# Recurrent mixer: gate matmuls in row-tile pairs, weights split by casting and accumulating DMAs, and a quarter of x turned by DMA

## The chip, the cores and the metric

One core of one Trainium2 chip runs the whole kernel. The metric is the device time of one execution in microseconds (us). Of the engines, PE is TensorE (PEld its weight loads), DVE VectorE, ACT ScalarE, POOL GpSimd, SP SyncE; DMAs are issued from the queues of SP, POOL and ACT.

## What is computed

Two layers, 512 positions, width 1024, everything in float32. Each layer is: half a SwiGLU feed-forward (inner width 2816), a token mixer, another half feed-forward, each behind an RMS norm and added to x. Layer 0's mixer is the Griffin recurrence, layer 1's a spatial gating unit. The change lies in layer 0's mixer and at the entry of the feed-forward behind it:

```python
def block_diag_linear(x, w, b):            # 16 heads of 64
    xh = x.reshape(bsz, s, h, dh)
    return (jnp.einsum('bshi,hij->bshj', xh, w) + b).reshape(bsz, s, h * dh)

def rg_lru(x, w_a, b_a, w_x, b_x, lam):
    gate_a = jax.nn.sigmoid(block_diag_linear(xf, w_a, b_a))
    gate_x = jax.nn.sigmoid(block_diag_linear(xf, w_x, b_x))
    log_a = -LRU_C * gate_a * jax.nn.softplus(-lam)
    a = jnp.exp(log_a)
    bx = xf * gate_x * jnp.sqrt(-jnp.expm1(2.0 * log_a))
    # h[t] = a[t] * h[t-1] + bx[t]

def recurrent_mixer(...):
    y, r = jnp.split(x @ w_in, 2, axis=-1)
    y = jax.nn.gelu(y)
    r = causal_depthwise_conv(r, conv_w, conv_b)      # width 4
    return (y * rg_lru(r, ...)) @ w_out
```

## The kernel before

**Three matmuls for one product.** Each float32 operand is split into a high and a low part of type float32r: hi is a ScalarE copy, lo a VectorE subtraction (source - hi). A product is then hi x hi + hi x lo + lo x hi, three matmuls into one PSUM bank (`mm3`, lines 247 to 250). Weights come from HBM by DMA into `raw` tiles (512 KB, ten buffers, `RAW_BUFS`), and `Sub.split` (from line 194) makes `whi` and `wlo` of them. The feed-forwards and output products use a seven-product scheme (named P1 to P7 and Q4) on quarters A11, A12, A21, A22 of the left side and sums of them (S1 to S4); these are `seven` and `out_blocks`. In that scheme a raw buffer is often changed in place: an accumulating DMA from POOL adds another weight block (`Raw.add`, line 161), either right after the load (`plus`, some blocks later) or after the first split (`then`).

**The order.** The program is a list `subs` of blocks; each has one raw buffer and its matmuls. The loop at the end of `trunk` goes through them. For block i it runs the accumulating loads that are due, the hook phase "pre", the split of block i + 3 (`SPLIT_AHEAD`), the phases "mid" and "rest", the loads for which buffers have come free (`load_more`), block i's matmuls, "end", the block's post-processing, and "late". Every engine runs its instructions in the order in which this loop issued them; the schedule is manual. So a hook at a block and phase fixes an instruction's place in its engine's queue.

**The recurrence** (`recurrent`, from line 1203). Its 1024 r columns and 1024 y columns are eight chunks of 128 each; below, r0 to r7 and y0 to y7 are their blocks. r0 to r3 come as two halves of 256 positions each, all first halves and then all second halves; r4 to r7, then y0 to y7, have 24 matmuls of 512 columns each. Behind a chunk r of the convolution's input there is, for chunk c: `rc` on ScalarE (the last tap and the bias, out of PSUM) and three taps on VectorE; a split of rc into hi and lo; the gate matmuls (`gate`); two sigmoids out of PSUM and a tanh (`sigmoids`, giving g and tl); `pr` = rc x gate_x on VectorE. Later hooks (`plan`) run the exponentials, `oma2` (two VectorE instructions on tl for 1 - a^2), the square roots, and the scans. Behind y there are gelus on ScalarE, and `yh` multiplies y by h.

**The gates before.** For two chunks of heads and each of the gates a and x a tile of 128 x 512 is cleared by a POOL memset, and 64 x 64 blocks are loaded on its block diagonal (`load_gate`, line 1206). The four tiles are split. Each chunk has one 128-row `mm3` per gate, half of whose weights are zeros: six matmuls of 512 columns, two banks. There are 48 of them.

**The output product and the norm.** y7 is followed by 14 blocks of 12 matmuls: P1, P5, P2 for the first cut of the left side, the same for the second, then P6, P3, P6, P3, P7, P7, Q4, Q4. When a quarter of x is final, `BlockNorm.quarter` arranges for its turning: `Group.stage` has TensorE transpose 128 x 128 pieces (eight for a quarter, line 294) into a PSUM bank, ScalarE evicts them with the norm's gains (`take`), and `parts` splits them. `BlockNorm` can do without TensorE for the quarters named in `cross`: `Group.rows` has ScalarE spread the 16-bit halves of x into planes (`pl`), SP transposes them by DMA (`dt`), ScalarE merges the halves, and the gains are applied in the later sums and splits. The feed-forwards around use it; the recurrence's `BlockNorm` has no `cross`. The first block of the next feed-forward (P1) needs A11's parts.

Of the kernel before, what the change touches and what calls it, by code (L numbers as in the profile page):

```python
# [14 lines left out]
P = 128  # L15
# [20 lines left out]
SPLIT_AHEAD = 3  # L36
SLOTS = 56
V_AT = 1, 7, 9, 10
WS_AT, WS_MERGE = 90, 8
# [36 lines left out]
def trunk(ctx: ExitStack, tc: tile.TileContext, a: dict, out: bass.AP):  # L76
# [57 lines left out]
    class Raw:  # L134


        halves = False

# [20 lines left out]

        def add(self, src):  # L160
            nc.gpsimd.dma_start(out=self.v, in_=src, accum_op=ALU.add)  # L161

# [11 lines left out]
    class Sub:  # L174
# [93 lines left out]
    def vcol(row):  # L268
        return vec[:, row : row + 1]
# [933 lines left out]
    def recurrent(w_in, w_out, norm):  # L1203
        gates = {}

        def load_gate(name, q):
            g = gates[name, q] = slot(name="gw")
            nc.gpsimd.memset(g, 0.0)
            gv = g.rearrange("p (c j) -> p c j", c=4)
            wv = a[f"rec_gate_{name}_w"][0, q * 8 : (q + 1) * 8].rearrange("(c two) i j -> two i c j", two=2)  # L1210
            for two in range(2):
                nc.sync.dma_start(out=gv[two * 64 : (two + 1) * 64, :, two * 64 : (two + 1) * 64], in_=wv[two])

        def split_gate(name, q):
            gates[name, q] = split(gates[name, q])

        at0 = len(subs)
        y0 = at0 + 12
        for n, (name, q) in enumerate((name, q) for q in range(2) for name in ("a", "x")):
            hook(at0 + (-9,-8,-2,-1)[n], "late", lambda name=name, q=q: load_gate(name, q))  # L1220
            hook(at0 + (-3,-2,3,4)[n], "mid", lambda name=name, q=q: split_gate(name, q))

        rc, ga, gx, tl, pr, ym = {}, {}, {}, {}, {}, {}

        def r_post(c, ps):
            n = now[0]
            g = n + (2 if c < 4 or c == 6 else 1)
            v = rc[c] = slot(name="rc")
# [27 lines left out]
            hook(n, "late", taps)  # L1256
            hook(n + 1, "mid", lambda: hl.extend(split(v)))
            hook(g, "end", gate)
# [56 lines left out]
        plan(1, "late", (exp_, 5, 6, 7), (oma2, 5, 6, 7))  # L1315
        plan(2, "rest", (sqrt, 5, 6, 7))
        plan(2, "late", (gelu, 0, 1, 2), (scan, 5, 6, 7))
        plan(3, "rest", (yh, 0, 1))
# [24 lines left out]
        def mk(c0, post, halves):  # L1343

            raw = raw_of(w_in[:, c0 : c0 + P].rearrange("(k p) c -> p k c", p=P), [P, KD, P])
            st = {}

# [8 lines left out]

            last = lambda: post(st[0])
            if not halves:
# [309 lines left out]
    def vec_rest():  # L1668

        nc.vector.memset(stage[:V_ROWS, :P], 0.0)  # L1670
        for src, r0, n in rows:
            flat = src.rearrange("h d -> (h d)") if len(src.shape) == 2 else src.rearrange("o h d -> (o h d)")
            nc.gpsimd.dma_start(out=stage[r0 : r0 + n, :P], in_=flat.rearrange("(n p) -> n p", p=P))

# [148 lines left out]
```

## Time and profile before

| | us |
|---|---|
| median of 3 runs | 1559.81 |
| lowest, highest | 1559.05, 1560.93 |
| the profiled execution | 1559.84 |
| its span | 1557.0 |
| TensorE busy in the span | 1549.4 |
| DVE, ACT, POOL busy | 1310.5, 1197.0, 245.6 |
| 48 gate matmuls, first and last start | 350.9 to 391.8 |

The granted TensorE clock is full throughout. In the profile's rows a start is in us from the span's start, and the number behind it is the recorded duration, in which matmuls overlap. In a row of groups, `out<-in xcount` stands for the tiles written and read and how often. A row of a tile's view gives the shortest, the median and the longest duration in ns.

### The profile page before, as it was taken

What the parts mean: (1) busy time and instruction counts of PE and PEld (TensorE: products, weight loads), DVE (VectorE), ACT (ScalarE), POOL (GpSimd) and SP (SyncE); (2) the same over time, 40 slices, a digit from 0 to 9 for tenths busy, and PEclk for the clock granted to TensorE, in tenths of its full rate; (3) what the DMA queues carried; (4) which work ended last, traced back from release to release, by engine and by line L of the source; (5) the groups of instructions that cost most, each with busy time, mean ns of one, the idle gap of its engine ahead of it and who ended that gap; (6) DMA issues with size and microseconds to landing.
All of it is one profiled execution on the core that took longest, in us unless ns stands there. A gap on an engine that the chain in (4) does not pass through costs nothing.

```text
span 1557.0 us, 20941 instructions
## 1 busy us (share of the span) xinstructions
PE 1549.4 (100%) x7237; PEld 1314.8 (84%) x7237; DVE 1310.5 (84%) x1792; ACT 1197.0 (77%) x1789; POOL 245.6 (16%) x220
## 2 busy tenths in 40 slices
PE   9999999999999999999999999999999999999998
PEld 7888888898888998888889988888888889888886
DVE  6977789888999787789897877798879997777998
ACT  7877786668778868786787787867887877777866
POOL 2111112300021111112211211122111111111120
PEclk9999999999999999999999999999999999999999
DMA  9988898953395988899987898989978869898994
GB/s 315 189 189 194 187 219 225 225 146 108 99 235 136 190 199 198 186 237 217 233 212 181 201 219 184 223 229 236 233 200 212 203 141 218 195 210 180 242 234 135
DMA packets 275098, 312.09 MB, mean 200 GB/s; under 512 B 117568, under 2 KB 155568, under 8 KB 274992
## 3 DMA queue, kind: packets, MB, share of 16 engines
q1 hardware_dynamic: 220704, 211.59, 47.6%
q0 software_dynamic: 52496, 97.33, 36.9%
q10 hardware_dynamic: 1792, 1.84, 0.4%
q8 instruction: 56, 0.92, 0.2%
q14 instruction: 50, 0.41, 0.1%
HBM read 282.39 MB, written 2.10 MB: 183 GB/s over the span
## 4 chain that ended last, share of the span: by engine, by line
PE 98%; DVE 1%; DMA 1%; issue 0%; ACT 0%; SPq 0%
PE A L484 15%; PE A L483 15%; PE A L485 15%; PE C L483 8%; PE C L485 8%; PE C L484 8%; PE B L484 4%; PE B L485 4%; PE B L483 4%; PE r L248 2%; PE r L250 2%; PE r L249 2%; PE Q L483 1%; PE Q L485 1%; PE Q L484 1%; PE p L963 1%
## 5 line engine op out<-in xcount | busy, mean ns | idle before, releaser
L110 DVE TENSOR_TENSOR wlo<-raw,whi 128x1024 fp32r<-128x1024 f32 (+2 forms) x567 | 651.1, 1152 | 208.8 <-ACT whi L119 203.6
L119 ACT ACTIVATE whi<-raw 128x1024 fp32r<-128x1024 f32 (+2 forms) x567 | 564.3, 1001 | 226.8 <-DVE raw L110 91.6
L483 PE MATMUL A<-whi,hi 128*128 128x512 f32 (+1 forms) x1104 | 420.9, 381 | 0.0
L484 PE MATMUL A<-whi,lo 128*128 128x512 f32 (+1 forms) x1104 | 419.4, 380 | 0.1
L485 PE MATMUL A<-wlo,hi 128*128 128x512 f32 (+1 forms) x1104 | 419.2, 380 | 0.0
L484 PEld LDWEIGHTS A<-whi,lo 128*128 128x128 f32 x1104 | 207.3, 188 | 36.0 <-DVE lo L110 1.0
L483 PEld LDWEIGHTS A<-whi,hi 128*128 128x128 f32 x1104 | 207.2, 188 | 36.0 <-ACT c L119 1.0
L485 PEld LDWEIGHTS A<-wlo,hi 128*128 128x128 f32 x1104 | 207.2, 188 | 35.6
L483 PE MATMUL C<-whi,hi 128*128 128x512 f32 (+1 forms) x608 | 231.5, 381 | 0.0
L484 PE MATMUL C<-whi,lo 128*128 128x512 f32 (+1 forms) x608 | 231.4, 381 | 0.0
L485 PE MATMUL C<-wlo,hi 128*128 128x512 f32 (+1 forms) x608 | 231.3, 380 | 0.0
L161 POOL DMA_DIRECT2D raw<-in_ffn_w_in_dram x100 | 120.7, 1207 | 697.4 <-DVE raw L110 331.5
L161 POOL DMA_DIRECT2D raw<-in_ffn_w_out_dram x73 | 83.8, 1195 | 318.3 <-DVE wlo L110 203.3
L110 DVE TENSOR_TENSOR raw<-raw,raw 128x1024 f32<-128x1024 f32 (+1 forms) x113 | 130.9, 1158 | 1.1
L484 PEld LDWEIGHTS C<-whi,lo 128*128 128x128 f32 x608 | 114.1, 188 | 20.4 <-DVE lo L110 0.4
L485 PEld LDWEIGHTS C<-wlo,hi 128*128 128x128 f32 x608 | 114.1, 188 | 19.9
L483 PEld LDWEIGHTS C<-whi,hi 128*128 128x128 f32 x608 | 114.1, 188 | 19.9
L110 DVE TENSOR_TENSOR lo<-a,hi 128x512 fp32r<-128x512 f32 (+1 forms) x180 | 116.3, 653 | 0.7 <-ACT hi L119 0.7
L119 ACT ACTIVATE c<-A 128x512 f32<-128x512 f32 (+1 forms) x150 | 81.8, 567 | 45.6 <-PE A L485 45.3
L119 ACT ACTIVATE hi<-a 128x512 fp32r<-128x512 f32 (+1 forms) x180 | 105.4, 595 | 14.4 <-DVE a L110 12.8
L484 PE MATMUL B<-whi,lo 128*128 128x512 f32 (+1 forms) x304 | 115.7, 381 | 0.1
L483 PE MATMUL B<-whi,hi 128*128 128x512 f32 (+1 forms) x304 | 115.7, 381 | 0.0
(189 smaller groups left out, 1974.0 us busy)
## 6 DMA issues: line engine op xcount, KB each, us to landing
raw<-in_ffn_w_in_dram SPq DMA_DIRECT2D x143, 512.0 KB, 5.6
raw<-in_ffn_w_out_dram SPq DMA_DIRECT2D x98, 512.0 KB, 6.0
raw<-in_ffn_w_in_dram POOLq DMA_DIRECT2D x76, 512.0 KB, 7.5
raw<-in_ffn_w_out_dram POOLq DMA_DIRECT2D x58, 512.0 KB, 8.6
raw<-in_ffn_w_in_dram SPq DMA_DIRECT2D x48, 384.0 KB, 4.3
raw<-in_sg_w_in_dram SPq DMA_DIRECT2D x20, 512.0 KB, 9.0
raw<-in_ffn_w_in_dram POOLq DMA_DIRECT2D x24, 384.0 KB, 6.2
raw<-in_rec_w_in_dram SPq DMA_DIRECT2D x16, 512.0 KB, 5.1
```

What stands on the lines that cost most here:

```text
L110: nc.vector.tensor_tensor(out=o, in0=x, in1=y, op=op)
L119: nc.scalar.activation(out=o, in_=x, func=f, **k)
L161: nc.gpsimd.dma_start(out=self.v, in_=src, accum_op=ALU.add)
L248: nc.tensor.matmul(ps, wh, xh, start=start, stop=False)
L249: nc.tensor.matmul(ps, wh, xl, start=False, stop=False)
L250: nc.tensor.matmul(ps, wl, xh, start=False, stop=stop)
L483: nc.tensor.matmul(ps, zh, wh, start=fresh and i == 0, stop=False, **k)
L484: nc.tensor.matmul(ps, zl, wh, start=False, stop=False, **k)
L485: nc.tensor.matmul(ps, zh, wl, start=False, stop=end, **k)
L963: nc.tensor.matmul(bank_of(half, s), z, (sub.lo if m == 2 else sub.hi)[:, q, :], start=left[2] == "2" and (h, q, m) == (0, 0, 0), stop=lef ...
```

## The change

- **Gates.** `load_gate` now fills one tile per chunk of four: for rows 0 to 63 (the even head) the columns hold gate a's block and then gate x's, for rows 64 to 127 (the odd head) gate x's and then gate a's. There are no zeros, no memset, and two tiles in place of four to load and to split. A chunk's gates are three pairs of matmuls; in a pair one matmul uses rows 0 to 63 and the other rows 64 to 127, each into its own bank. Each bank then holds half of both gates, so there are four sigmoids on 64 partitions in place of two on 128, and gate x's bias is loaded with its halves exchanged.
- **Places.** `GATE` puts the gates of most chunks a block later. Chunks 4 to 7 have hi of rc made by VectorE (`OWN_HI`). The first exponentials come one block later; those of chunks 5 to 7, their roots and scans also move by a phase or a block.
- **Casting loads.** For r4 to r7 and y0 to y5 a second DMA from POOL reads the same weights again and casts them into a tile `rawhi`; ScalarE's copy `whi` is dropped and VectorE makes wlo from raw and rawhi. Each such block holds two of the ten buffers, and rawhi until its matmuls are done, so later loads come later.
- **Accumulating loads.** For y6 and y7 (`BELOW`) only rawhi is loaded. Two blocks later ScalarE writes -hi into `rawlo`, and an accumulating DMA from POOL adds the weights: VectorE has no part in it.
- **x's quarter A11** behind the recurrence goes the way of `cross`.

```diff
+GATE = (3, 3, 3, 2, 2, 2, 2, 2)
+OWN_HI = 4
+BELOW = {6: 2, 7: 2}
...
         def load(self):
             _, k, c = self.shape
+            if self.below:
+                self.h, self.l = (rawp.tile([P, 1024], F32R, tag="raw", name=nm(x)).rearrange("p (k c) -> p k c", k=k)
+                                  for x in ("rawhi", "rawlo"))
+                live.update(((self, "hi"), (self, "lo")))
+                nc.gpsimd.dma_start(out=self.h, in_=self.src)
+                pending.append((now[0] + self.below, self))
+                pending.sort(key=lambda p: p[0])
+                return
...
+            if self.cast:
+                self.h = rawp.tile([P, 1024], F32R, tag="raw", name=nm("rawhi")).rearrange("p (k c) -> p k c", k=k)
+                live.add((self, "hi"))
+                nc.gpsimd.dma_start(out=self.h, in_=self.src)
...
         def add(self, src):
+            if self.below:
+                act(self.l, f32(self.h), AF.Copy, scale=-1.0)
+                nc.gpsimd.dma_start(out=self.l, in_=self.src, accum_op=ALU.add)
+                return
...
+            if self.raw.below:
+                self.hi, self.lo = self.raw.h, self.raw.l
+                return
             src = self.raw.v
+            if self.raw.cast:
+                self.hi = self.raw.h
+                _, k, c = src.shape
+                self.lo = wp.tile([P, 1024], F32R, tag="wlo", name=nm("wlo")).rearrange("p (k c) -> p k c", k=k)
+                tt(self.lo, src, f32(self.hi), ALU.subtract)
+                self.raw.used()
+                return
...
-            g = n + (2 if c < 4 or c == 6 else 1)
+            g = n + GATE[c]
...
             def gate():
-                for name in "ax":
-                    pg = bank("gate")
-                    wh, wl = gates[name, c // 4]
-                    cs = slice((c % 4) * P, (c % 4 + 1) * P)
-                    mm3(pg, wh[:, cs], wl[:, cs], hl[0], hl[1], True, True)
-                    pss.append(pg)
+                pss.extend(bank("gate") for _ in range(2))
+                cs = slice((c % 4) * P, (c % 4 + 1) * P)
+                for m in range(3):
+                    for two in range(2):
+                        rows = slice(two * 64, (two + 1) * 64)
+                        nc.tensor.matmul(pss[two], gates[c // 4][m == 2][rows, cs], hl[0][m == 1][rows, :],
+                                         start=m == 0, stop=m == 2)
                 hl.clear()
...
-                for dst, brow in ((ga, V_GA), (gx, V_GX)):
-                    dst[c] = slot(name="g")
-                    act(dst[c], pss.pop(0), AF.Sigmoid, bias=vcol(brow + c))
+                for dst, brow, n in ((ga, V_GA, 0), (gx, V_GX, 1)):
+                    g = dst[c] = slot(name="g")
+                    for two in range(2):
+                        o = (two ^ n) * 64
+                        act(g[two * 64 : (two + 1) * 64], pss[two][o : o + 64], AF.Sigmoid, bias=vcol(brow + c)[o : o + 64])
...
-        plan(-2, "rest", (exp_, 0, 1, 2, 3, 4), (oma2, 0, 1))
+        plan(-1, "rest", (exp_, 0, 1, 2, 3, 4), (oma2, 0, 1))
...
-    recurrent(a["rec_w_in"][0], a["rec_w_out"][0], BlockNorm(V_F2, True, wait=("A12",)))
+    recurrent(a["rec_w_in"][0], a["rec_w_out"][0], BlockNorm(V_F2, True, wait=("A12",), cross={"A11": (((1, "pre"), (4, "rest"), (5, "rest")), ((1, "rest"), (5, "mid"), (6, "mid")))}))
...
-        while loaded < n and len(live) < RAW_BUFS:
+        while loaded < n and len(live) < RAW_BUFS - raws[loaded].cast:
```

Three places show how instructions move. First TensorE, at chunk 1's gate; before, between the last matmuls of a block r and the first of the next (gate is the PSUM bank, its operands are the split gate weights and the split rc):

```order
L250 MATMUL r_3547<-zh_3086,wlo_3391 128x512
L248 MATMUL gate_3572<-hi_3486,hi_3112 128x512
L249 MATMUL gate_3572<-lo_3487,hi_3112 128x512
L250 MATMUL gate_3572<-hi_3486,lo_3113 128x512
L248 MATMUL gate_3576<-hi_3486,hi_3134 128x512
L249 MATMUL gate_3576<-lo_3487,hi_3134 128x512
L250 MATMUL gate_3576<-hi_3486,lo_3135 128x512
L248 MATMUL r_3603<-zh_3058,whi_3429 128x512
```

The same engine and kind of place after the change:

```order
L279 MATMUL r_3512<-zh_3082,wlo_3377 128x512
L1273 MATMUL gate_3537<-hi_3414,hi_3110 128x512
L1273 MATMUL gate_3538<-hi_3414,hi_3110 128x512
L1273 MATMUL gate_3537<-lo_3415,hi_3110 128x512
L1273 MATMUL gate_3538<-lo_3415,hi_3110 128x512
L1273 MATMUL gate_3537<-hi_3414,lo_3111 128x512
L1273 MATMUL gate_3538<-hi_3414,lo_3111 128x512
L277 MATMUL r_3570<-zh_3054,rawhi_3000 128x512
```

The six matmuls now alternate between two banks, each reading 64 rows of the same tiles; the block behind them reads rawhi from the casting load in place of whi. Second ScalarE, from the last roots (tl) through the gelus (y); before:

```order
L119 ACTIVATE tl_3861<-tl_3861 128x512
L119 ACT_TABLE_LOAD
L119 ACTIVATE y_3949<-r_3799 128x512
L119 ACTIVATE y_3951<-r_3874 128x512
L119 ACTIVATE y_3953<-r_3924 128x512
L119 ACTIVATE whi_3964<-raw_3398 128x1024
L119 ACTIVATE hi_4001<-a_850_3968 128x512
L119 ACTIVATE whi_4005<-raw_3437 128x1024
L119 ACTIVATE y_4009<-r_3976 128x512
```

After:

```order
L122 ACTIVATE y_3942<-r_3849 128x512
L122 ACTIVATE y_3944<-r_3912 128x512
L122 ACTIVATE rawlo_3847<-rawhi_3846 128x1024
L122 ACTIVATE hi_3992<-a_838_3959 128x512
L122 ACTIVATE y_3997<-r_3967 128x512
L122 ACTIVATE hi_4005<-a_845_3999 128x512
L122 ACTIVATE whi_4037<-raw_3908 128x1024
```

The splits of y6 and y7 (the two whi rows) have gone; y7's copy into rawlo stands where y6's split stood, right behind the third gelu. Third POOL's queue through the recurrence; before:

```order
L1208 MEMSET gw_3154 128x512
L1208 MEMSET gw_3182 128x512
L161 DMA raw_3545<-in_rec_w_out_dram 128x2x512
L161 DMA raw_3741<-in_rec_w_out_dram 128x2x512
L161 DMA raw_3974<-in_rec_w_out_dram 128x2x512
L161 DMA raw_3545<-in_rec_w_out_dram 128x2x512
```

After, from the casting load of y5 on:

```order
L166 DMA rawhi_3713<-in_rec_w_in_dram 128x8x128
L155 DMA rawhi_3783<-in_rec_w_in_dram 128x8x128
L155 DMA rawhi_3846<-in_rec_w_in_dram 128x8x128
L178 DMA rawlo_3784<-in_rec_w_in_dram 128x8x128
L178 DMA rawlo_3847<-in_rec_w_in_dram 128x8x128
L180 DMA raw_3910<-in_rec_w_out_dram 128x2x512 x2
L180 DMA raw_4048<-in_rec_w_out_dram 128x2x512
```

Twelve casting loads and two accumulating ones stand ahead of the first accumulating load of the output product, and the second of those (`raw_4048`, P5's second cut) now stands behind both loads into P5's first buffer (`raw_3910`).

More of the change, by code (lines that the diff above doesn't have):

```diff
@@ L134, in trunk @@
     class Raw:
-        halves = False
+        halves = cast = below = False
         def __init__(self, src, shape, plus=None, wait=2):
@@ L1204, in recurrent, with load_gate, split_gate @@
         gates = {}
[L1206 to L1208 removed]
+        def load_gate(q):
+            g = gates[q] = slot(name="gw")
             gv = g.rearrange("p (c j) -> p c j", c=4)
[L1210 to L1215, printed above, removed]
+            for n, name in enumerate("ax"):
+                wv = a[f"rec_gate_{name}_w"][0, q * 8 : (q + 1) * 8].rearrange("(c two) i j -> two i c j", two=2)
+                for two in range(2):
+                    o = (two ^ n) * 64
+                    nc.sync.dma_start(out=gv[two * 64 : (two + 1) * 64, :, o : o + 64], in_=wv[two])
+        def split_gate(q):
+            gates[q] = split(gates[q])
         at0 = len(subs)
         y0 = at0 + 12
[L1219 to L1221 removed]
+        for q in range(2):
+            hook(at0 + (-9, -2)[q], "late", lambda q=q: load_gate(q))
+            hook(at0 + (-3, 3)[q], "mid", lambda q=q: split_gate(q))
         rc, ga, gx, tl, pr, ym = {}, {}, {}, {}, {}, {}
@@ L1256, in r_post, with parts @@
             hook(n, "late", taps)
-            hook(n + 1, "mid", lambda: hl.extend(split(v)))
+            def parts():
+                hi, lo = slot(F32R, "hi"), slot(F32R, "lo")
+                if c < OWN_HI:
+                    act(hi, v, AF.Copy)
+                else:
+                    nc.vector.tensor_copy(hi, v)
+                tt(lo, v, f32(hi), ALU.subtract)
+                hl.append((hi, lo))
+            hook(n + 1, "mid", parts)
             hook(g, "end", gate)
@@ L1345, in mk @@
             raw = raw_of(w_in[:, c0 : c0 + P].rearrange("(k p) c -> p k c", p=P), [P, KD, P])
+            raw.cast = not halves
+            raw.below = BELOW.get(c0 // P, 0)
             st = {}
@@ L1355, in mm_of, with last @@
                 return mm
-            last = lambda: post(st[0])
+            def last():
+                live.difference_update(((raw, "hi"), (raw, "lo")))
+                post(st[0])
             if not halves:
@@ L1672, in vec_rest @@
             flat = src.rearrange("h d -> (h d)") if len(src.shape) == 2 else src.rearrange("o h d -> (o h d)")
-            nc.gpsimd.dma_start(out=stage[r0 : r0 + n, :P], in_=flat.rearrange("(n p) -> n p", p=P))
+            v = flat.rearrange("(n p) -> n p", p=P)
+            if r0 == V_GX:
+                for o in (0, 64):
+                    nc.gpsimd.dma_start(out=stage[r0 : r0 + n, o : o + 64], in_=v[:, 64 - o : 128 - o])
+            else:
+                nc.gpsimd.dma_start(out=stage[r0 : r0 + n, :P], in_=v)
     def vec_rest_t():
```

10 lines of the change are left out of this document (7 added, 3 removed).

## The prediction

> **What bounds the kernel now.** I read the page first (busy time, chain), then what TensorE waits for, then its instructions in order of time.
>
> ```profile
> span 1557.0 us, 20941 instructions
> PE 1549.4 (100%) x7237; PEld 1314.8 (84%) x7237; DVE 1310.5 (84%) x1792; ACT 1197.0 (77%) x1789; POOL 245.6 (16%) x220
> ...
> PE 98%; DVE 1%; DMA 1%; issue 0%; ACT 0%; SPq 0%
> ```
> ```profile
> PE warm L1660 <- DVE warm L1655: 1.3, 1, 1.3
> ```
>
> TensorE is busy throughout, holds 98% of the chain that ended last, and its only listed wait is the warm-up's. So the time is the sum of TensorE's matmul intervals, and anything else counts only where it makes TensorE stand. A busy TensorE is still not a measure of an instruction's price, since matmuls overlap in the records; the price is the distance from start to start. The timeline of TensorE around the first gate shows it:
>
> ```profile
> 350.83 0.28 PE L250 MATMUL r<-zh,wlo 128*128 128x256 f32 x1
> 350.95 0.40 PE L248 MATMUL gate<-hi,hi 128*128 128x512 f32 x1
> 351.18 0.40 PE L249 MATMUL gate<-lo,hi 128*128 128x512 f32 x1
> ...
> 352.33 0.28 PE L248 MATMUL r<-zh,whi 128*128 128x256 f32 x1
> ```
>
> A 512-column matmul is recorded with 0.39 us, but the next starts 0.23 us later; a 256-column one takes 0.12 us. The six matmuls of one gate run from 350.95 to 352.33: 1.38 us, and all eight gates 11.0 us.
>
> **The gates.** After the change a gate is three pairs. A pair's two matmuls each use 64 of the 128 rows and write different banks. If the two run at once, a pair costs one 512-column interval, 0.23 us. It also needs two weight loads, and the 256-column matmul above shows that a load with its matmul goes through in 0.12 us: two loads set a floor of 0.24 us per pair. That makes 3 x 0.24 = 0.72 us per gate and 5.8 us for eight: 5.2 us saved at best. The trace has no 64-row matmul, so a price is unknown: what going from whole-array to half-array matmuls and back costs. The most it should cost is the overlap of neighbours, 0.39 - 0.23 = 0.16 us. There are 14 such switches, not 16, since the gates of chunks 2 and 3 stand next to each other. That is 0 to 2.2 us, and with no row nearer to either end I take half, 1.1 us. The saving is then 5.2 - 1.1 = 4.1 us.
>
> The Trainium skill, page TensorEngine Tiling (Array Packing), Key Properties, states that a change of the tiling mode drains TensorE; no run here shows it yet. By that rule the whole 2.2 us is paid and the sum below is 1.1 us worse.
>
> **The turned quarter.** The chain of waits in order of time has the transposes of x's quarter A11:
>
> ```profile
> 457.50 0.87 PE e L294 x8
> ```
>
> Those eight transposes leave TensorE: 0.9 us. What replaces them is on ScalarE, SyncE's queue and VectorE:
>
> ```profile
> L119 ACT ACTIVATE pl<-x x16: 613/614/632, 737.5 to 1090.2; 128x512 uint16<-128x512 uint16 x16
> ```
> ```profile
> L119 ACT ACTIVATE a<-dt x82: 682/1172/1197, 59.0 to 1461.7; 128x1024 uint16<-128x1024 uint16 x70, 128x512 uint16<-128x512 uint16 x12
> ```
> ```profile
> L119 ACT ACTIVATE a<-e,vec x39: 452/466/532, 9.4 to 1235.6; 128x256 f32<-128x256 f32 x39
> ```
>
> ScalarE gets four planes (4 x 0.61) and two merges (2 x 1.17), 4.8 us, and loses four evictions (4 x 0.47 = 1.9): about 3 us more in the 16 us before the next feed-forward. The split of A11 stays, one or two blocks later than now, and is due a block (2.7 us) after it is queued. ScalarE is not full there (windows below: 29.1 of 40 us), so I put this at nothing; if its backlog reaches that block, TensorE stands for up to 1 us. The two transfers on SyncE's queue stand behind weight loads and have three blocks to land.
>
> **Loads and splits.** The windows of the recurrence's second half and of its output product, each with the busy time of TensorE, weight load, VectorE, ScalarE and GpSimd:
>
> ```profile
> 390.00:430.00 40.00, 40.00 (x178) 33.14 (x177) 38.47 (x56) 28.70 (x40) 3.10 (x3) 1.00 0.40 105
> 430.00:470.00 40.00, 40.00 (x190) 33.37 (x189) 37.79 (x52) 29.09 (x50) 8.98 (x8) 1.00 0.94 223
> ```
>
> VectorE is full from 390 us on (38.5 of 40), the DMA engines are idle more than half of the time until 430 us (0.40), ScalarE has 11 us to spare. ScalarE loses 12 copies to whi (1.07, the last row of its timeline below) and six smaller splits. It gets 16 more sigmoids, since one on 64 partitions handles as many elements per partition as one on 128 (I price it like those in the next row), and two copies to rawlo. That is 12 x 1.07 = 12.8 and the splits out, 16 x 0.69 + 2 x 1.07 = 13.2 in: no gain, no harm. The 12 cast loads of 0.5 MB use DMA time that is idle. GpSimd's four memsets and the gate's second weight split fall away beside other work and are worth nothing.
>
> ```profile
> L119 ACT ACTIVATE g<-gate,vec x16: 672/686/700, 356.1 to 399.3; 128x512 f32<-128x512 f32 x16
> ```
>
> What can cost is the last recurrence block, y7. Its low part is no longer made by VectorE: ScalarE writes -hi into rawlo, then GpSimd queues an accumulating DMA, and TensorE's third matmul needs it. On ScalarE the copy stands behind the three gelus, the gelus behind the roots of chunks 5 to 7, the roots behind VectorE. VectorE's and ScalarE's rows of that stretch now:
>
> ```profile
> 387.65 1.22 DVE L110 TENSOR_TENSOR wlo<-raw,whi 128x1024 fp32r<-128x1024 f32 x1
> 388.79 0.68 DVE L110 TENSOR_TENSOR pr<-rc,g 128x512 f32<-128x512 f32 x1
> ...
> 407.76 0.69 DVE L116 SCALAR_TENSOR_TENSOR tl<-a,tl 128x512 f32<-128x512 f32 x1
> 408.37 1.22 DVE L110 TENSOR_TENSOR wlo<-raw,whi 128x1024 fp32r<-128x1024 f32 x1
> ```
> ```profile
> 372.50 1.27 ACT L119 ACTIVATE g<-gate,vec 128x512 f32<-128x512 f32 x2
> 373.65 0.74 ACT L119 ACTIVATE tl<-g,lru_c 128x512 f32<-128x512 f32 x1
> ...
> 374.92 1.28 ACT L119 ACT_TABLE_LOAD   x1
> 376.21 3.18 ACT L119 ACTIVATE g<-g,lru_nc 128x512 f32<-128x512 f32 x5
> ...
> 384.61 0.78 ACT L119 ACTIVATE rc<-r,vec 128x512 f32<-128x512 f32 x1
> ...
> 410.44 1.58 ACT L119 ACTIVATE y<-r 128x512 f32<-128x512 f32 x3
> 411.88 1.07 ACT L119 ACTIVATE whi<-raw 128x1024 fp32r<-128x1024 f32 x1
> ```
>
> And TensorE's first matmul of y1, and its first of the output product, which follows y7:
>
> ```profile
> 392.05 0.39 PE L248 MATMUL r<-zh,whi 128*128 128x512 f32 x1
> ```
> ```profile
> 430.13 0.39 PE L483 MATMUL A<-whi,hi 128*128 128x512 f32 x1
> ```
>
> Between them lie seven blocks of 24 matmuls, 5.44 us each. So r6 ends at 392.05 less y0 and r7 (10.9) and three gates (4.1): 377.0. After the change it has four gates of 0.86 (6.9 us over eight) ahead of it in place of five of 1.38, and ends at 373.6. The new order puts the five exponentials between r6's rc and r7's rc on ScalarE, so the latter starts after rc 0.7, a wait for the gate 0.2, four sigmoids 2.3 (two take 1.15 from start to start), a tanh 0.6, a table load 1.3 and the exponentials 3.1: 8.2 us, at 381.8, 2.8 us sooner than the 384.6 above. VectorE's stretch from the end of y3's wlo to the last tl takes 408.4 - 388.8 = 19.6 us now; in the new order it also holds a cast and two more products pr (at most 0.6 each from start to start) and y5's wlo (1.1): 22.5 us. It starts 2.8 us sooner with the rc that it waits for, and ends at 388.8 - 2.8 + 22.5 = 408.5; the gelus end 3.5 us behind it as now, and rawlo of y7 is ready for its DMA at 413.1.
>
> How long such a DMA takes is bounded by the accumulating loads of today (POOLq) and by what small rows cost the plain ones (SPq; rec_w_in comes in rows of 512 B, rec_w_out in rows of 2 KB); three rows of the DMA view of 290 to 480 us, then one of the page's issues, then the spread over all loads of line 161:
>
> ```profile
> raw<-in_rec_w_in_dram SPq DMA_DIRECT2D x14, 512.0 KB, 5.0
> raw<-in_rec_w_out_dram SPq DMA_DIRECT2D x10, 512.0 KB, 3.9
> ...
> raw<-in_rec_w_out_dram POOLq DMA_DIRECT2D x8, 512.0 KB, 6.5
> ```
> ```profile
> raw<-in_ffn_w_out_dram POOLq DMA_DIRECT2D x58, 512.0 KB, 8.6
> ```
> ```profile
> DMA to landing us min/median/max: 5.0/7.5/13.7
> ```
>
> 6.5 to 8.6, and 1.1 for the small rows (5.0 - 3.9): 7.6 to 9.7 us, so it lands between 420.7 and 422.8. y7 starts at 430.1 - 5.4 = 424.7 now and at 424.7 - 4.1 = 420.6 after the change, and its first rawlo matmul is due two matmuls later, at 421.0. TensorE stands for 0 to 1.8 us; I take 0.7. With the largest landing seen (13.7) it is 5.8. y6's rawlo is made some 15 us before its use and is not late. The output product's weights now start to load seven blocks later, and the accumulating load of P5's second cut queues on GpSimd behind another that waits for VectorE; by the same prices it may be up to 1 us late, but a stand at y7 gives it that time, so the two are not added.
>
> The Trainium skill, page DMA: Bandwidth & Descriptors, Anatomy of one DMA, fits a GpSimd-issued DMA as 2.0 us + bytes / 436 GB/s, an estimate of 3.2 us for 512 KB. This case's accumulating loads do not agree (6.5 to 8.6 us). By the page y7 would not wait and the sum would be 0.7 us better.
>
> **The sum.** -4.1 (gates) - 0.9 (transposes) + 0.7 (y7) = -4.3 us. The profiled execution took 1559.84 us, 2.8 us more than its span, and the three runs have their median at 1559.81, so the same base serves: 1555.5 us. A measurement here tells 0.2% apart, 3.1 us: faster is below 1556.7, slower above 1562.9.
>
> **The rivals.**
>
> (1) The pairs do not run at once: each 64-row matmul takes its own 0.23 us. For it: no row of the trace shows two matmuls side by side. Against: they use different rows and banks. Then the gates stay at 11.0 us plus 0 to 2.2 for the switches, y7 comes too late to wait, and the transposes' 0.9 remains: 1558.9 to 1561.1 us, no change.
>
> (2) The pairs work and the accumulating loads are late: y7, or P5's second cut, waits 3 to 6 us (landings of 11 to 14 us, which the spread above contains). For it: the DMA share of 0.94 from 430 us on. Against: the share is 0.40 where y7's load runs. Net -2 to +1: 1557.8 to 1560.8 us, no change.
>
> (3) Slower: 512-byte casting and accumulating DMAs take some 17 us, twice the 8.6. Then y6's cast, whose buffer comes free with y3's wlo (386.0), lands at 403; ScalarE stands on it with the last sigmoids, exponentials and gelus queued behind, y7's rawlo is ready at 417 and lands at 434, 13 us late: net +8, 1568 us. Below about 15 us per load it does not come to 1562.9. For it: four times as many rows per load, and none of 512 B in today's accumulating loads. Against: small rows cost the plain load only 1.1 us.
>
> **How the numbers follow.** My forecast's case (pairs side by side, y7 waits under 2 us) spans 1553.7 (no switch cost, no wait: -5.2 - 0.9) to 1556.7: chance 0.61. Rival 1: 0.17. Rival 2: 0.15. Rival 3: 0.07. The range goes from 1553.6 to 1559.8, which takes in the forecast and over half of rivals 1 and 2. Faster 0.61, no change 0.32, slower 0.07.
>
> **What would show it.** Right: in the timeline a gate's two matmuls start together or within 0.12 us, and a gate spans 0.7 to 1.0 us from its first matmul to the next block's; no e row near 452 us; the list of TensorE's waits shows r waiting on the DMA of rawlo, 0 to 2 us, and nothing else of size. Wrong: gate matmuls 0.23 us apart; a wait of TensorE on rawhi, on a bank behind the sigmoids, or on A11 at the first block of the next feed-forward; rawlo landing more than 11 us after its issue.

## The result: slower, and the profile after

The changed kernel takes 1573.63 us in the median of six runs (1570.06 to 1580.25), the kernel before 1559.06 in six. The ratio is 1.0097, 95% interval 1.007 to 1.0123: slower by 1%, where -4.3 us was forecast. The profiled execution took 1570.06 us, 10.2 more than the one before; it is the fastest of the six runs, so what the others have on top of it (3.6 us at their median) is in no trace. The page and TensorE's waits after:

```profile
span 1568.4 us, 20976 instructions
...
PE   9999999999979999999999999999999999999998
...
PE 68%; DVE 2%; DMA 1%; issue 1%; ACT 1%; POOL 0%; DVEq 0%; POOLq 0%; ACTq 0%
```
```profile
PE C L512 <- ACT hi L122: 8.3, 1, 8.3
PE r L279 <- DMA rawlo<-in_rec_w_in_dram: 1.4, 1, 1.4
...
PE e L323 <- ACT a L122: 0.7, 1, 0.7
```

TensorE's share of the chain fell from 98 to 68%. Followed back from the end, the chain leaves TensorE at one long wait and can be followed no further than a load issued at 416.3 us, so most of the lost share is the 416 us ahead of it, which are not in the chain at all. The slice with a 7 is that wait: 8.3 us on bank C, which is P5's second cut.

The gates, in the timeline of TensorE (a row with x2 is two matmuls, 2 to 4 ns apart):

```profile
353.80 0.28 PE L279 MATMUL r<-zh,wlo 128*128 128x256 f32 x1
354.01 0.50 PE L1273 MATMUL gate<-hi,hi 64*128 64x512 f32 x2
354.35 0.40 PE L1273 MATMUL gate<-lo,hi 64*128 64x512 f32 x2
354.59 0.39 PE L1273 MATMUL gate<-hi,lo 64*128 64x512 f32 x2
354.90 0.50 PE L277 MATMUL r<-zh,rawhi 128*128 128x512 f32 x1
355.24 0.39 PE L278 MATMUL r<-zl,rawhi 128*128 128x512 f32 x1
355.47 0.39 PE L279 MATMUL r<-zh,wlo 128*128 128x512 f32 x1
```

The pairs run side by side, 0.23 us per pair. But four distances are too long: 0.21 in place of 0.12 ahead of the gate, 0.34 behind its first pair, 0.31 ahead of the next block and 0.34 behind its first matmul. That is 0.40 us for one visit to half-array matmuls and back. With seven such places (chunks 2 and 3 stand together) the gates take 8 x 0.70 + 7 x 0.40 = 8.4 us in place of 11.0: 2.6 us saved.

The big wait, first on TensorE, then in the chain that leads to it:

```profile
440.08 0.39 PE L514 MATMUL A<-wlo,hi 128*128 128x512 f32 x1
448.74 0.80 PE L512 MATMUL C<-whi,hi 128*128 128x512 f32 x1 [8.27 <-ACT hi L122]
449.81 0.79 PE L513 MATMUL C<-whi,lo 128*128 128x512 f32 x1 [0.28 <-DVE lo L113]
450.40 0.63 PE L514 MATMUL C<-wlo,hi 128*128 128x512 f32 x1
450.83 0.63 PE L512 MATMUL C<-whi,hi 128*128 128x512 f32 x1
```
```profile
430.33 13.47 DMA raw<-in_rec_w_out_dram
443.90 1.06 ACT whi L122
444.99 1.11 DVE wlo L113
446.13 1.28 DVE lo L113 x2
447.42 0.60 DVE a L113
```

Read the chain downwards. The accumulating load of P5's second cut is issued at 430.33 and lands 13.5 us later. ScalarE stands for it with `whi` at the head of its queue, VectorE stands for ScalarE, and the sum `a` from which the block's left side is split comes last. GpSimd's and ScalarE's queues show why the load was issued so late:

```profile
415.42 1.55 POOL L178 DMA_DIRECT2D rawlo<-in_rec_w_in_dram  x1 [13.51 <-ACT rawlo L122]
416.32 1.86 POOL L180 DMA_DIRECT2D raw<-in_rec_w_out_dram  x1
429.60 2.43 POOL L180 DMA_DIRECT2D raw<-in_rec_w_out_dram  x2 [11.41 <-DVE wlo L113]
```
```profile
426.97 1.06 ACT L122 ACTIVATE whi<-raw 128x1024 fp32r<-128x1024 f32 x1 [4.29 <-DMA raw<-in_rec_w_out_dram]
...
443.90 1.06 ACT L122 ACTIVATE whi<-raw 128x1024 fp32r<-128x1024 f32 x1 [9.90 <-DMA raw<-in_rec_w_out_dram]
```

GpSimd stood 13.5 us for y7's copy into rawlo, with the first accumulating load of rec_w_out behind it. That load landed at 427.0, so the first cut's split ended near 429.2, and only then could the queued second load of the first cut go, and behind it (the second DMA in the row at 429.60) the one of the second cut. Before the change, the load of the second cut left GpSimd's queue 42 us sooner:

```profile
387.91 1.20 POOL L161 DMA_DIRECT2D raw<-in_rec_w_out_dram  x1 [19.47 <-DVE rc L116]
```

The wait has a tail. TensorE's next matmuls are 0.43 us apart in place of 0.23. The windows behind the wait (the last four columns are GpSimd's busy time, the granted clock, the DMA share and GB/s):

```profile
440.00:448.70 8.70, 0.47 (x3) 0.04 (x1) 3.71 (x5) 3.69 (x6) 1.98 (x2) 0.81 0.94 220
448.70:450.40 1.70, 1.39 (x2) 0.79 (x3) 1.70 (x3) 1.70 (x2) 0.45 (x1) 0.50 0.91 118
450.40:452.40 2.00, 2.00 (x6) 1.59 (x5) 2.00 (x4) 0.69 (x2) 1.20 (x1) 0.53 1.11 193
452.40:456.00 3.60, 3.60 (x17) 2.95 (x16) 3.60 (x6) 1.41 (x2) 0.00 (x0) 1.00 1.01 218
```

After the stand the granted clock is half for about 3.7 us, which (with 0.3 us of waiting for lo) costs 2.1 us more.

The sum from the distances between TensorE's starts, matmul by matmul against the trace before: -2.5 (gates) - 0.7 (A11's transposes) + 1.6 (y7) + 8.4 (P5) + 2.1 (its tail) + 1.9 (at the transposes of the other quarters) = +10.8. The last matmul starts 11.4 us later and the span is 11.4 us longer; the other 0.6 us are small steps elsewhere. The two device times differ by 1.2 us less than the spans, because 2.8 us of the execution before lie outside its span and 1.7 us of the one after.

### The profile page after: what moved, and what is told of

Its sections match the earlier page's. It is cut to its first block, busy times and chain, and to the rows that moved or that the text cites. A ratio compares the mean times of both kernels' runs of the same rounds, so it can differ in the third digit from the quotient of the medians.

```text
span 1568.4 us, 20976 instructions
## 1 busy us (share of the span) xinstructions
PE 1549.5 (99%) x7229; PEld 1308.3 (83%) x7229; DVE 1309.6 (84%) x1796; ACT 1199.3 (76%) x1793; POOL 258.2 (16%) x231
## 4 chain that ended last, share of the span: by engine, by line
PE 68%; DVE 2%; DMA 1%; issue 1%; ACT 1%; POOL 0%; DVEq 0%; POOLq 0%; ACTq 0%
PE A L513 12%; PE A L512 12%; PE A L514 12%; PE C L513 7%; PE C L514 6%; PE C L512 6%; PE B L512 3%; PE B L514 3%; PE B L513 3%; PE Q L513 1%; PE Q L512 1%; PE Q L514 1%; DMA raw<-in_rec_w_out_dram 1%; DVE wlo L113 1%; PE e L323 1%
## 5 line engine op out<-in xcount | busy, mean ns | idle before, releaser
L113 DVE TENSOR_TENSOR wlo<-raw,whi 128x1024 fp32r<-128x1024 f32 (+2 forms) x555 | 636.4, 1150 | 220.9 <-ACT whi L122 218.9
L122 ACT ACTIVATE whi<-raw 128x1024 fp32r<-128x1024 f32 (+2 forms) x555 | 551.1, 999 | 240.0 <-DVE raw L113 90.7
L514 PE MATMUL B<-wlo,hi 128*128 128x512 f32 (+1 forms) x304 | 115.7, 380 | 0.0
```

The source lines that it names most:

```text
L113: nc.vector.tensor_tensor(out=o, in0=x, in1=y, op=op)
L122: nc.scalar.activation(out=o, in_=x, func=f, **k)
L514: nc.tensor.matmul(ps, zh, wl, start=False, stop=end, **k)
```

## The experiments

The first theory, formed from this profile, was the queue theory: P5's load comes late because of its place in GpSimd's queue, and the rest is harmless. Its rivals were that the DMA engines are full, that the new places of the gates or A11's new path fill VectorE and ScalarE, and that the pairs themselves cost more than they save. Each median below has the ratio to the kernel before, from runs on the same chip, with its 95% interval; the medians of the kernel before were 1559.4 to 1560.3 us there, and the ratio need not be the quotient of two medians.

**pairs_only.** The gates alone. Of the changed kernel this keeps `load_gate`, `gate`, `sigmoids` and the exchanged bias; against it:

```diff
-GATE = (3, 3, 3, 2, 2, 2, 2, 2)
+GATE = (2, 2, 2, 2, 1, 1, 2, 1)
-OWN_HI = 4
+OWN_HI = 8
-            raw.cast = not halves
-            raw.below = BELOW.get(c0 // P, 0)
```

(the old `plan` rows, and no `cross` for A11, too.) Expected:

> The kernel before with the gates as row-tile pairs and nothing else of the change (old places of gates and exponentials, no casting or accumulating loads in the recurrence, A11 turned by TensorE). Queue theory (the loss comes from P5's second cut, whose accumulating load is issued late behind another on GpSimd's queue): no wait of TensorE above 1 us in the output product; the gates alone remain, and as the trace of after has about 0.40 us of switching at each of 7 places, they save 8 x (1.38 - 0.70) - 7 x 0.40 = 2.6 us: 1557.2 us. With the switch price of the prediction (1.1 us in all) it is 1555.7. Rival, the pairs themselves are the loss (bank or sigmoids late): over 1562.

Measured: 1567.78 us, 1.0052 (1.0035 to 1.0068). The pairs alone lose 8 us, and the queue theory cannot say why. TensorE's waits:

```profile
PE gate L1273 <- ACT hi L122: 3.5, 3, 1.9
PE gate L1273 <- DVE lo L113: 1.6, 3, 1.1
```

And a row of ScalarE's timeline there:

```profile
373.10 2.79 ACT L122 ACTIVATE g<-gate,vec 64x512 f32<-64x512 f32 x4
```

Four sigmoids on 64 partitions take 2.79 us, where two on 128 took 1.27 (the prediction's row at 372.50). ScalarE gets 11 us more work between 350 and 410 us, hi of rc comes late behind it, and the next gate waits. The two rows are 5.1 us; the rest of the 8 us and of the gates' saving goes in smaller waits and in lower clock (0.95 from 350 to 400 us, in the windows below).

**no_casts.** The changed kernel with one raw buffer per block again:

```diff
-            raw.cast = not halves
-            raw.below = BELOW.get(c0 // P, 0)
```

> The kernel after without casting and accumulating loads in the recurrence: pairs, the new places and A11 by the DMA crossbar stay, every block has one raw buffer again. Queue theory and bandwidth theory alike: rec_w_out's loads start near 358 us again in place of 388, no stall at P5's second cut, 2.6 us from the gates and 0.9 from the transposes: 1556.3 us. Rival, the new places or A11's new path fill VectorE and ScalarE in the output product and cause the stall: it stays, over 1566.

Measured: 1572.56 us, 1.0085 (1.006 to 1.011), 16 us over the forecast. P5's wait is gone (0.3 us), as the first reading had it, and yet nothing is won:

```profile
PE r L277 <- ACT whi L122: 3.6, 2, 1.8
PE e L323 <- ACT a L122: 2.6, 2, 1.9
```

Now y blocks wait for `whi`, the copy that the casting loads had taken from ScalarE. So ScalarE's sigmoids are a cost of their own, for which the later places and the casting loads pay; the queue theory was only a part. (Of this profiled execution 4.5 us more lie at three matmuls from 1044 us on, in the spatial part. The traces of few_casts, r_casts_below and y7_plus_nocross below lose 3, 2 and 1 us at the same place; no run explains it.)

**two_sigmoids** tests that directly: pairs_only, but

```diff
-                    for two in range(2):
-                        o = (two ^ n) * 64
-                        act(g[two * 64 : (two + 1) * 64], pss[two][o : o + 64], AF.Sigmoid, bias=vcol(brow + c)[o : o + 64])
+                    act(g, pss[n], AF.Sigmoid, bias=vcol(brow + c))
```

> Pairs alone (as in pairs_only), but with two sigmoids of 128 partitions per chunk in place of four of 64; the halves of gates a and x are then mixed up, which only this kernel does. New theory (ScalarE): a sigmoid takes 0.68 us whatever its partitions, so the pairs cost ScalarE 16 x 0.69 = 11 us, in 350 to 400 us where it has 45 of 50 us busy; hi of rc comes late, and the gates wait for it 5.1 us plus lower clock. Then this kernel has no waits at the gates and saves 2.6 us: 1557 us. Rival (the gates simply come too early in the old places because TensorE is faster): waits of 3 us or more stay, 1562 or more.

Measured: 1558.3 us, 0.9993 (0.9984 to 1.0003). The gates' waits shrink from 5.1 to 0.7 us and 9.5 us come back. ScalarE's 16 additional sigmoids are what the pairs cost; the rival, early places, is out. (With its gates mixed up this kernel is no version to use, and even it gains no more than 0.1% over the kernel before, within the interval.) Busy time in 350 to 400 us (TensorE, its weight loads, VectorE, ScalarE, GpSimd), of pairs_only and then of two_sigmoids:

```profile
350.00:400.00 50.00, 44.10 (x209) 32.66 (x208) 37.33 (x50) 45.06 (x63) 2.41 (x2) 0.95 0.40 101
```
```profile
350.00:400.00 50.00, 48.71 (x242) 37.77 (x242) 44.31 (x58) 42.31 (x60) 2.41 (x2) 1.00 0.41 107
```

**plus_ahead** and **y7_earlier** test the queue, each by one number of the changed kernel: the block at which P5's second accumulating load is queued, and that of y7's copy.

```diff
-                    raw[11, ci] = new(0, 0, (0, 1))
+                    raw[11, ci] = new(0, 0, (0, 1), 0 if far(ci) and ci == 1 else 2)
```

> The kernel after with one number changed: the accumulating load of P5's second cut is queued on GpSimd ahead of the second accumulating load of the first cut (which waits for VectorE), not behind it. The same loads, bytes and buffers. Queue theory: it is issued near 418 us in place of 430.3 and lands before 435; ScalarE's copy does not stand for it, the 8.4 us wait, the 2.0 us of lower clock behind it and some 1.5 us at the transposes behind go: 1558 to 1560 us, with y7's 1.6 us left. Bandwidth theory (the DMA engines are full from 420 us on, in whatever order): the wait moves to another block of the output product and 1566 us or more remain.

```diff
-BELOW = {6: 2, 7: 2}
+BELOW = {6: 2, 7: 1}
```

> The kernel after with BELOW for y7 set to 1: ScalarE's copy into rawlo stands a block earlier, ahead of the last sigmoids and the gelus. Queue theory: GpSimd, which stood for that copy until 415.4, issues rawlo of y7 near 401 and the first accumulating load of rec_w_out near 405; TensorE's 1.6 us at y7 go, P5's first cut is split 4 us sooner, and the load of the second cut behind it goes out near 426: the wait there falls from 8.4 to some 4 us, 1562 to 1565 us in all. Bandwidth theory: only y7's 1.6 us go, 1568.5.

Measured: plus_ahead 1571.82 us, 1.0084 (1.0053 to 1.0115); y7_earlier 1567.4 us, 1.0036 (1.002 to 1.0051). In plus_ahead the load goes out at 416.9 and lands at 431.0, and P5's wait falls to 0.5 us, so the place in the queue was what made it. But the time did not move beyond its interval, as the bandwidth theory had it, and the wait went to the next transposes:

```profile
PE e L323 <- ACT a L122: 8.6, 2, 8.3
PE A L512 <- DVE x L119: 1.9, 1, 1.9
```

ScalarE's merges of A11 wait 8.8 us there for the crossbar's DMAs (the crossbar stands for the transposing DMA in these texts), which land 12.3 and 15.4 us after their issue, and the evictions of the next transposes stand behind the merges. In y7_earlier y7's wait is gone and P5's is 3.5 us, both as expected, and the transposes wait 3.0 us, which was not; the time lies between what the two theories gave.

**cross_only** and **no_cross** separate A11's new path: the one is the kernel before with it, the other the changed kernel without it.

```diff
-    recurrent(a["rec_w_in"][0], a["rec_w_out"][0], BlockNorm(V_F2, True, wait=("A12",)))
+    recurrent(a["rec_w_in"][0], a["rec_w_out"][0], BlockNorm(V_F2, True, wait=("A12",), cross={"A11": (((1, "pre"), (4, "rest"), (5, "rest")), ((1, "rest"), (5, "mid"), (6, "mid")))}))
```

> The kernel before with x's quarter A11 turned by the DMA crossbar and nothing else. Theory: ScalarE's merges stand for the transposing DMA (7 to 15 us to landing), the evictions of the next transposes stand behind them, and TensorE waits at the second transposes of a quarter, 1 to 3 us: 1560 to 1563 us. The prediction's price (nothing for the new path, 0.9 saved): 1558.9 us.

> The kernel after with A11 turned by TensorE again. Theory: the waits at the transposes (0.9 and 0.75 us, more in slower runs) go, 0.9 us of transposes come back; the 8.4 us at P5's second cut and the 2.0 us of lower clock stay: 1569 to 1570 us, and the spread of the runs is smaller. Rival (A11's planes and merges are what makes ScalarE late at P5 too): under 1563.

Measured: cross_only 1562.77 us, 1.0017 (1.0005 to 1.0029), by itself a loss; no_cross 1571.76 us, 1.0071 (1.0056 to 1.0086), some 2 us over its forecast, with P5's wait at 9.1 us. So in the changed kernel, whose ratio has an overlapping interval, A11's path by itself makes no difference that can be told. In cross_only the rows of ScalarE say what stands for what (this execution took 1566.53 us, 3.8 above the median, so its waits are longer than the usual ones):

```profile
469.31 1.17 ACT L119 ACTIVATE a<-dt 128x1024 uint16<-128x1024 uint16 x1 [2.77 <-DMA dt<-pl]
470.39 0.82 ACT L119 ACTIVATE a<-e,vec 128x256 f32<-128x256 f32 x2
```
```profile
463.02 1.04 PE L294 MATMUL e<-ident,x 128*128 128x128 f32 x8
...
471.26 0.80 PE L294 MATMUL e<-ident,x 128*128 128x128 f32 x4 [4.47 <-ACT a L119]
```

The merge (a<-dt) stands for the DMA, the eviction (a<-e) behind it frees the bank, and TensorE's next four transposes start 0.05 us after that eviction's end.

**cross_sooner** tests whether the landing or ScalarE's work is the price: cross_only, with A11 final and its DMAs issued a block sooner, and the merges in the same blocks (their hooks count from the block where A11 is final, so each goes up by one; not shown).

```diff
-        gs = out_blocks(w_out, 0, [2, 2], 1.0, norm, order, own=True, soon=soon, p2_lag=2)
+        gs = out_blocks(w_out, 0, [2, 2], 1.0, norm, order, own=True, soon=soon, p2_lag=1)
```

> The kernel cross_only with x's quarter A11 made final one block sooner (2.7 us), its planes and transposing DMAs with it, while ScalarE's merges stay in their blocks. Theory (the loss is ScalarE standing for the crossbar's landing, which took 10.4 to 11.3 us there): the merges' 4.9 us of waiting fall to under 1, TensorE's 5.1 us at the transposes to under 1: 1559 to 1560 us, under cross_only by 3 us. Rival (ScalarE's 3 us of additional work is the loss): stays at 1562 to 1563.

Measured: 1561.16 us, 1.0004 (0.9986 to 1.0021). No merge waits for a DMA any more, though ScalarE's additional work is still there, and of the 5.1 us at the transposes none is left on ScalarE:

```profile
PE A L483 <- DVE x L116: 1.4, 1, 1.4
...
PE C L484 <- DVE lo L110: 0.7, 1, 0.7
PE e L294 <- DVE x L116: 0.4, 2, 0.2
```

So the waits at the transposes came from the landing. The time does not show it as plainly: it lies between the two forecasts, and its interval overlaps that of cross_only. There is a new wait of 1.4 us on bank A, behind VectorE's update of x, which the edit also moves; the loss is no longer measurable, and neither is a gain.

**y7_plus_nocross** mends all three faults found: the edits of y7_earlier and plus_ahead, and A11 turned by TensorE as in no_cross.

> The kernel after with three things mended: y7's copy a block earlier, the accumulating load of P5's second cut ahead of the one that waits for VectorE, and A11 turned by TensorE. Theory (late accumulating loads and the crossbar's landing are all that costs): no wait over 1 us in the output product and behind it; 2.6 us from the gates: 1557.2 us, 0.2% under the kernel before. Bandwidth theory (the loads of w_out come in half the time and the DMA engines are full): some block waits 3 us or more, 1560 or more.

**grouped** is that kernel with fewer switches between whole and half arrays:

```diff
-GATE = (3, 3, 3, 2, 2, 2, 2, 2)
+GATE = (4, 3, 3, 2, 2, 2, 3, 2)
```

> The kernel y7_plus_nocross with the gates of chunks 0 and 6 a block later, so that they stand next to those of 1 and 7: 5 places with gates in place of 7. If a place costs 0.40 us of switching, as the trace of after has it, this saves 0.8 us of TensorE's intervals, to be seen in the distances from start to start; in the time, 1559.5 against 1560.3, unless the later sigmoids make something else late. If the switches cost what the prediction took (0.08 each), it saves 0.3.

Two more, both made from no_cross, keep casting loads only where ScalarE needs them. **few_casts**:

```diff
-BELOW = {6: 2, 7: 2}
+BELOW = {}
...
-            raw.cast = not halves
+            raw.cast = not halves and (c0 >= D or c0 < 2 * P)
```

> The kernel after with casting loads for r4 to r7, y0 and y1 only (6 in place of 10), no accumulating loads for y6 and y7, and A11 turned by TensorE. Six copies whi less on ScalarE are meant to pay for most of the 11 us of the 16 sigmoids, while the buffers come free three to four blocks sooner than in after. If both theories hold (ScalarE's 11 us, and late buffers): no wait over 1 us anywhere, 1557 to 1558 us. If six copies are too few, TensorE waits for whi of y6 and y7 (3.6 us in no_casts): 1560 to 1562. If the buffers are still too late, it waits at P5's second cut, over 1562.

**r_casts_below**:

```diff
-BELOW = {6: 2, 7: 2}
+BELOW = {6: 2, 7: 1}
...
-            raw.cast = not halves
+            raw.cast = not halves and c0 >= D
```

> The kernel after with casting loads for r4 to r7 only, the accumulating loads of y6 and y7 kept (y7's copy a block earlier), and A11 turned by TensorE. What the runs so far say, put together: y6 and y7 need no split of ScalarE and VectorE (the wait of few_casts), the casts of y0 to y5 hold no second buffer, so that the loads of w_out go out three blocks sooner than in after, and no merge stands for the crossbar. If these are all the causes, no wait over 1 us is left and the gates' 2.6 us remain: 1557 us, against 1559 to 1560 before. If ScalarE, which makes six more copies whi than in after, is still too full, a y block waits for whi, 1 to 3 us: 1558.5 to 1560.5, no gain.

Measured: y7_plus_nocross 1560.34 us, 0.9997 (0.9989 to 1.0006); grouped 1561.03 us, 0.9993 (0.9979 to 1.0007); few_casts 1566.44 us, 1.0035 (1.0018 to 1.0051); r_casts_below 1563.49 us, 1.0012 (1.0001 to 1.0023). All four miss their forecasts: the first by 3.1 us, grouped by 1 to 1.5 us (on its chip the kernel before took 0.8 us more as well), and the last two by 3 us or more, even against what was forecast for a late ScalarE. Mending the three faults takes the whole loss away, 13 us, and leaves no gain that can be measured. The largest waits that are left, of y7_plus_nocross, grouped, few_casts and r_casts_below:

```profile
PE C L513 <- DVE lo L113: 0.9, 2, 0.5
PE A L513 <- DVE lo L113: 0.8, 1, 0.8
PE A L512 <- DVE x L119: 0.5, 1, 0.5
```
```profile
PE C L512 <- ACT hi L122: 1.1, 1, 1.1
PE gate L1273 <- ACT g L122: 0.9, 1, 0.9
```
```profile
PE r L277 <- ACT whi L122: 3.4, 1, 3.4
PE C L513 <- DVE lo L113: 1.8, 2, 1.2
...
PE A L513 <- DVE lo L113: 1.2, 1, 1.2
```
```profile
PE C L513 <- DVE lo L113: 2.3, 3, 1.2
PE C L512 <- ACT hi L122: 1.7, 1, 1.7
```

In y7_plus_nocross no wait is over 1 us, as its theory said, and the gates' 2.5 us are still there at 450 us. By 459 us they are gone: waits of 0.8, 0.4 and 0.5 us behind VectorE's lo and x, with the longer distances around them, take 2.9 us. No run moves VectorE's work there, so what a mended kernel still lacks is read from this one trace and not tested. In grouped each of the five places still costs 0.4 us, so the two places fewer did save 0.8. But four gates stand in two neighbouring blocks, and TensorE waits 0.9 us for a bank that ScalarE's sigmoids have yet to read; with this wait the gates save 1.9 us in place of 2.5. With fewer casting loads ScalarE is late again, at y7 or in the output product. No version made here beats the kernel before by more than a measurement can tell.

## Why the prediction was wrong

**The step that failed** is the last sentence of the part on loads: "the accumulating load of P5's second cut queues on GpSimd behind another that waits for VectorE; by the same prices it may be up to 1 us late, but a stand at y7 gives it that time", so that the sum has nothing for it. The place was named and the size was wrong: 8.4 us, and 2.1 more by its tail of lower clock. The prediction does not show how it came to 1 us. Redone with its upper price and the other stretches of the chain from the trace after, this is an estimate: y7's copy at 413.1, 0.9 to the issue of the first cut's load, 9.7 to its landing, 3.4 to the issue of the second cut's load, 9.7, and 4.9 to a matmul that was due at 440.3; it comes out 1.4 us late. So two loads in a row were not enough to make the wait; the links were mis-sized. The copy was ready 2.3 us later, at 415.4, and the two loads took 10.6 us (416.3 to 427.0) and 13.5 us (430.3 to 443.8), 0.9 and 3.8 over the bound. These are the other 7.0 us. That the chain is what made the wait, plus_ahead and y7_earlier show: 0.5 us are left with the load ahead in the queue, 3.5 with the copy a block earlier. Rival 2 came closest, with landings of 11 to 14 us, a wait of 3 to 6 and a chance of 0.15; 3 to 6 is about what one such landing adds, and it had no term for the clock.

**The second failure** is "I put this at nothing" for A11's new path. Its reasons were that ScalarE is not full and that the two transfers have three blocks (8.2 us) to land. They took 7.0 and 7.2 us in the changed kernel's trace, but 10.4 and 11.3 in cross_only and up to 15.4 in plus_ahead. What counts is not A11's own due time but what is queued behind the merge on ScalarE: the eviction that frees a bank for the next quarter's transposes. Alone this cost 3.3 us between the medians, and the eight transposes that left TensorE gave back 0.7 us by the distances, not 0.9.

**The gates.** That pairs run at once was right (rival 1 is out). The switch was mis-sized: 0.40 us per place, 2.8 us in all, above the bound of 2.2 and far from the 1.1 taken. The overlap of recorded durations did not bound it. The Trainium skill, page TensorEngine Tiling (Array Packing), Key Properties, has a change of tiling mode drain TensorE. The measured 0.40 us per place agree with a cost at each change, though half of it shows a matmul later, behind the first pair and behind the first whole matmul.

**ScalarE's balance**, "no gain, no harm", held for the whole change: 16 sigmoids at 0.68 us in, the copies out (ScalarE's busy time went from 1197.0 to 1199.3 us, with A11's merges in it). What the prediction did not draw from it is that the casting loads are no gain of the change but the payment for its pairs (pairs_only: +8 us without them), and that they bring the late loads.

**y7** was expected at 0.7 us, in a range of 0 to 1.8, and measured 1.6, inside the range; the copy into rawlo ended only at 415, and its load landed 8.8 us after issue, within the 7.6 to 9.7.

**Rival 3**'s premise, 17 us per small-row DMA, was wrong (accumulating loads of rec_w_in took 6.2 and 8.8 us, the casts 5.2 in the median). Slower came by another way.

What stays open: why the same accumulating loads of rec_w_out took 10.2 us in the median and up to 13.5 after, 6.5 before. Much of it goes with loads that are under way together. Of the eight before, seven were issued with at most 1.3 us of another GpSimd load still to go and took 5.6 to 7.9 us; the eighth, issued 0.7 us behind another, took 9.7. After, six of eight were issued with over 4 us of another still to go and took 7.4 to 13.5; the other two took 5.8 and 10.2. The DMA share was 1.09 and 1.10 in the two windows of 5 us from 435 to 445 us, and 1.01 and 0.96 before, which fits as well, but no run changed the overlap or the share alone. Nor were casting loads run without pairs, and the 3.6 us between the profiled execution and the median have no trace.

## What to carry to other kernels

A load that is queued behind a waiting one is priced by the whole chain in front of it, each link with its own landing, and not by its own duration; ask of every engine queue what stands behind an instruction that waits for a DMA. Halving a matmul's rows saved TensorE time, but the evictions on ScalarE took as long on 64 partitions as on 128, so a result whose halves lie in two banks cost twice there. When several measures each remove work from an engine and the time rises, run each of them alone first: here two were a loss by themselves, and the third, which was not run alone, paid for one of them.

## What the runs showed of the hardware

A sigmoid from PSUM took 0.683 us on 64 partitions (pairs_only) and 0.686 on 128 (the kernel before), with 512 columns each: half the partitions saved no time.

After a stand of 8.3 us TensorE's granted clock was 0.50 to 0.53 for 3.7 us, so that this wait cost a quarter more than it lasted. The tail is no fixed share of the wait: after 9.1 us in no_cross the clock was 0.50 for 6.1 us (to 455.5), after 3.4 us in few_casts for 3.3 us (427.2 to 430.5), and after two stands of 1.7 and 0.6 us close together in r_casts_below for about 3 us (442.5 to 445.5). The Trainium skill, page TensorE: Matmul & The Clock Gate, Part 1, describes half clock after an idle window of some 3.4 us until a busy window of that length has passed. The 3.7 us agree with the length of such a window; the two short stands of r_casts_below, which are not 3.4 us of idle time even together, were enough all the same.

Two matmuls on different halves of the rows, into different banks, started 2 to 4 ns apart, and a pair took 0.23 us, the distance of one matmul on all rows. Going from whole-array to half-array matmuls and back cost 0.40 us a visit, the same for one gate as for two.

A transposing DMA of a half quarter took 7.0 to 15.4 us to land: 7.0 and 7.2 in the changed kernel, 7.8 and 8.3 in cross_sooner, 10.4 and 11.3 in cross_only, 12.3 and 15.4 in plus_ahead. That this goes by what else the queues moved is likely but not shown.
